# Both feed-forwards of a two-layer diffusion backbone: gate and up as seven block products, activations through DRAM, down summed over all chunks in PSUM

## The chip, the cores and the metric

The kernel runs on one core of a Trainium2 chip. A core has a matrix engine, TensorE (PE), three elementwise engines, VectorE (DVE), ScalarE (ACT) and GpSimd (POOL), and an engine, SyncE (SP), whose queue issues all DMAs of this kernel. The metric is the device time of one execution in microseconds; the median of the runs counts.

## What is computed

The reference has two layers over 512 latent tokens and 256 context tokens of width 1024. Layer 0 mixes the tokens by differential attention, layer 1 by grouped-query attention; only the latent tokens are the output, so layer 1 has no feed-forward for the context. All numbers are float32. What matters here:

```python
def modulate(t, shift, scale):
    return t * (1 + scale) + shift

def swiglu(t, w_gu, w_down):
    gate, up = jnp.split(t @ w_gu, 2, axis=-1)
    return (jax.nn.silu(gate) * up) @ w_down
...
        mod = (cond_lat @ ada_w[i] + ada_b[i])[:, None, :]
        modc = (cond_ctx @ ada_w[i] + ada_b[i])[None, None, :]
        sh1, sc1, g1, sh2, sc2, g2 = jnp.split(mod, 6, axis=-1)
...
        x = x + g1 * y
        x = x + g2 * swiglu(modulate(rmsnorm(x, norm2_g[i]), sh2, sc2), ffn_w_gu[i], ffn_w_down[i])
        if not last:
            xc = xc + cg1 * yc
            xc = xc + cg2 * swiglu(modulate(rmsnorm(xc, norm2_g[i]), csh2, csc2), ffn_w_gu[i], ffn_w_down[i])
```

The hidden width is 2816, which is 22 chunks of 128.

## The kernel before

**Number format.** Each float32 operand of a large product is split into a high part (a cast to fp32r) and a low part (the rest), and a product is three matmuls: high x high, high x low, low x high (mm3, L99). So each weight that comes from DRAM is cast by ACT and subtracted by POOL (split, L85: guh/gul for gate and up, dh/dl for down, woh/wol for the output projection). Names that end in h or l are high and low parts.

**Order.** A scheduler sets the order of every engine's instructions from the program; each engine then works through its own queue in that order. Raw weights land in a pool of three buffers (rawp, 8 KB in each partition), which gate/up, down, output-projection and adaLN weights share; SP issues their loads in order.

**Attention's end in layer 0.** The heads' outputs (po) are normed on ACT, DVE, POOL and, for the mean, PE (pm). Six of eight heads are spilled to DRAM and read back (ol), cast and split into oT0. The first half of the output projection's weights is split ahead of the attention's end, and the sums over the six spilled heads for four of the six token blocks (pso0p) are made early, copied to SBUF (pac) and added later; then come the sums pso. After the last column half of a token block is added to x (L365), norm_a, norm_t (transposes pt on PE) and norm_m (L312; modulation on DVE L322 and ACT L324, cast L327, low part L328) give the transposed, modulated tokens h2 (h3 in layer 1).

**Feed-forward (ffn, L369).** The loop runs over chunks. stage (L419) loads 1 MB of gate and up columns and splits it. gu_mm (L426) multiplies: for gate and for up, 8 blocks of 128 rows, three matmuls each, that is 48 weight blocks of 128x128, each against 512 latent columns (psgu) and, in layer 0, 256 context columns (psgc). ACT applies silu, DVE multiplies by up (L479), ACT casts, DVE takes the low part (L493); the activations a stay in SBUF. Every two chunks (PIECE) down (L375) makes, for each token block and each half of the 1024 columns, six matmuls into a bank psd; DVE multiplies it by the gate (L386, xd) and adds it to x (L387). That is 11 pairs of chunks x 12 sums in layer 0 and x 8 in layer 1, 220 evictions of two operations.

**adaLN of layer 1.** Its scale and shift vectors are sums over 1024 rows, made on DVE in layer 0's feed-forward: 16 operations at L223 and 112 at L225, 128x512 each (adacc<-adaw), one column block at a time between the products (ada_job, L395). Those of layer 0 for the second half of the layer are made on PE (ps_ada) inside the attention.

## Time and profile before

| | us |
|---|---|
| runs: median (lowest to highest of 3) | 1748.15 (1746.62 to 1748.38) |
| span of the profiled execution | 1742.5 |
| PE busy in it | 1657.0 (95%) |
| DVE busy | 1237.5 (71%) |
| ACT busy | 673.0 (39%) |
| POOL busy | 767.6 (44%) |

The span runs from the first to the last instruction that the profile shows; a run's time is the device's and holds a little more. Matmuls are pipelined: a matmul of 512 columns is recorded with 0.39 us while the next starts 0.23 us after it, so the starts are what is to be read. The feed-forward of layer 0 lies between about 520 and 1137 us of the span, that of layer 1 between about 1365 us and the end.

### The profile page before, as it was taken

The numbers are of one execution on the slowest core, as the hardware profiler recorded it, in microseconds if no ns is written. First come the engines' busy times: TensorE is split into PE (matmuls) and PEld (weight loads), VectorE is DVE, ScalarE is ACT, GpSimd is POOL, SyncE is SP. The second block draws the span as 40 slices with busy tenths as digits, with TensorE's granted clock in tenths as the row PEclk, the third lists the DMA queues.
The fourth block names the chain that finished last, engine by engine and source line by source line (L and its number), as shares of the span: only waits on it lengthen the run. The fifth ranks groups of instructions, "written<-read, shape, count | busy, mean of one in ns | idle before, by whom it ended". The sixth has DMA issues, their size and how long they took to land.

```text
span 1742.5 us, 23575 instructions
## 1 busy us (share of the span) xinstructions
PE 1657.0 (95%) x8934; PEld 1403.6 (81%) x8934; DVE 1237.5 (71%) x2016; ACT 673.0 (39%) x1491; POOL 767.6 (44%) x702
## 2 busy tenths in 40 slices
PE   5899999989998999999999999999999999999998
PEld 2789899975778888887777888778897888888887
DVE  4777888877484488878777555798883467677676
ACT  4667767677444121111211022364673522222120
POOL 2687666664645242223232233174435344354340
PEclk8899999999999999999999999999999999999999
DMA  8311111129523133355333221021203133233311
GB/s 303 102 55 38 46 46 58 34 75 336 195 73 121 49 121 111 107 169 169 122 119 99 73 73 40 25 74 48 73 25 120 36 105 103 73 97 99 95 49 49
DMA packets 162435, 165.81 MB, mean 95 GB/s; under 512 B 5097, under 2 KB 120186, under 8 KB 162322
## 3 DMA queue, kind: packets, MB, share of 16 engines
q1 hardware_dynamic: 162322, 164.31, 29.5%
q8 instruction: 70, 1.15, 0.3%
q14 instruction: 43, 0.35, 0.1%
HBM read 159.81 MB, written 4.48 MB: 94 GB/s over the span
## 4 chain that ended last, share of the span: by engine, by line
PE 68%; DVE 18%; ACT 4%; DMA 4%; POOL 3%; issue 2%; SPq 0%; DVEq 0%; ACTq 0%; POOLq 0%
PE psgu L433 24%; PE psgc L433 5%; PE psd L100 5%; PE psd L102 5%; PE psd L101 5%; DVE adacc L225 3%; DMA adaw<-in_ada_w_dram 3%; PE psp L100 2%; PE psp L102 2%; PE psp L101 2%; DVE adacc L223 2%; DVE x L387 2%; DVE xd L386 1%; PE pso L100 1%; PE pso L102 1%
## 5 line engine op out<-in xcount | busy, mean ns | idle before, releaser
L93 POOL TENSOR_TENSOR gul<-gu,guh 128x2048 fp32r<-128x2048 f32 x44 | 211.6, 4809 | 419.6 <-ACT guh L86 419.6
L386 DVE TENSOR_TENSOR xd<-psd,gate 128x512 f32<-128x512 f32 x220 | 151.1, 687 | 202.7 <-PE psd L102 202.5
L387 DVE TENSOR_TENSOR x<-x,xd 128x512 f32<-128x512 f32 x220 | 274.4, 1249 | 5.5
L86 ACT CAST guh<-gu 128x2048 fp32r<-128x2048 f32 x44 | 83.9, 1906 | 403.8 <-PE psgu L433 234.4
L91 POOL TENSOR_TENSOR dl<-wd,dh 128x1024 fp32r<-128x1024 f32 x44 | 120.9, 2768 | 146.1 <-ACT dh L86 146.1
L433 PE MATMUL psgu<-h3latl,guh 128*128 128x512 f32 (+1 forms) x384 | 144.5, 377 | 1.1 <-POOL h3latl L328 1.1
L433 PE MATMUL psgu<-h3lath,gul 128*128 128x512 f32 (+1 forms) x384 | 144.4, 376 | 0.0
L433 PE MATMUL psgu<-h3lath,guh 128*128 128x512 f32 (+1 forms) x384 | 144.3, 377 | 0.0
L433 PE MATMUL psgu<-h2lath,guh 128*128 128x512 f32 (+1 forms) x368 | 142.1, 386 | 0.0
L433 PE MATMUL psgu<-h2lath,gul 128*128 128x512 f32 (+1 forms) x368 | 141.8, 385 | 0.0
L433 PE MATMUL psgu<-h2latl,guh 128*128 128x512 f32 (+1 forms) x368 | 141.8, 385 | 0.0
L100 PE MATMUL psd<-dh,ah 128*128 128x512 f32 x264 | 106.0, 402 | 16.2 <-DVE xd L386 12.1
L102 PE MATMUL psd<-dh,al 128*128 128x512 f32 x264 | 104.8, 397 | 0.0
L101 PE MATMUL psd<-dl,ah 128*128 128x512 f32 x264 | 104.5, 396 | 0.0
L433 PE MATMUL psgc<-h2ctxh,gul 128*128 128x256 f32 x352 | 100.2, 285 | 0.4 <-POOL gul L93 0.4
L433 PE MATMUL psgc<-h2ctxh,guh 128*128 128x256 f32 x352 | 100.1, 284 | 0.0
L433 PE MATMUL psgc<-h2ctxl,guh 128*128 128x256 f32 x352 | 99.6, 283 | 0.0
L225 DVE SCALAR_TENSOR_TENSOR adacc<-adaw,cond,adacc 128x512 f32<-128x512 f32 x112 | 97.5, 896 | 1.3
L100 PE MATMUL psp<-dwh,h0lath 128*128 128x384 f32 x256 | 88.9, 347 | 7.6 <-DVE vl L97 7.6
L101 PE MATMUL psp<-dwl,h0lath 128*128 128x384 f32 x256 | 88.9, 347 | 0.0
L102 PE MATMUL psp<-dwh,h0latl 128*128 128x384 f32 x256 | 88.8, 347 | 0.0
L433 PEld LDWEIGHTS psgu<-h3latl,guh 128*128 128x128 f32 x384 | 72.2, 188 | 15.8 <-POOL h3latl L328 1.3
(389 smaller groups left out, 4669.1 us busy)
## 6 DMA issues: line engine op xcount, KB each, us to landing
adaw<-in_ada_w_dram SPq DMA_DIRECT2D x48, 1024.0 KB
gu<-in_ffn_w_gu_dram SPq DMA_DIRECT2D x88, 512.0 KB
wd<-in_ffn_w_down_dram SPq DMA_DIRECT2D x22, 1024.0 KB
dw<-in_diff_w_in_dram SPq DMA_DIRECT2D x48, 256.0 KB
x<-in_x_dram SPq DMA_DIRECT2D x8, 512.0 KB
wo<-in_diff_w_out_dram SPq DMA_DIRECT2D x4, 1024.0 KB
gw<-in_gqa_w_in_dram SPq DMA_DIRECT2D x4, 1024.0 KB
wo<-in_gqa_w_out_dram SPq DMA_DIRECT2D x4, 1024.0 KB
```

What stands on the lines that cost most here:

```text
L86: S.copy(hi, src)
L91: G.tensor_sub(lo[:, ns], src[:, ns], hi[:, ns])
L93: G.tensor_sub(lo[:, :, ns], src[:, :, ns], hi[:, :, ns])
L100: PE.matmul(ps, lhi, rhi, start=start, stop=False)
L101: PE.matmul(ps, lhi, rlo, start=False, stop=False)
L102: PE.matmul(ps, llo, rhi, start=False, stop=stop)
L223: V.tensor_scalar(acc, w[:, k, :], c, None, op0=ALU.mult)
L225: V.scalar_tensor_tensor(acc, w[:, k, :], c, acc, op0=ALU.mult, op1=ALU.add)
L386: V.tensor_mul(tmp, ps, gates[g][:, s, cs])
L387: last_v[0] = V.tensor_add(xt[tb][:, cs], xt[tb][:, cs], tmp)
L433: last[0] = PE.matmul(o, w_[:, k, us], act.t[kind][x_].k(k, sl_), start=(k == 0 and x_ == 0 and w_ is whi), stop=(k == KC - 1 and w_ is wlo))
```

## The change

**Gate and up** become ffn_up. The weights of a chunk are four blocks of 512 rows x 128 columns (two halves of the rows, gate and up), and the tokens four blocks as well: two halves of the rows and two halves of the tokens (three blocks of 128 in layer 0, [4, 5, 0] and [1, 2, 3], where 4 and 5 are the context; two in layer 1). In place of eight block products there are seven, each of one weight form with one token form; each is 4 x 3 = 12 matmuls of 384 columns (256 in layer 1). The class Forms makes the token forms b11, b21, b22 and t1 to t4 once; prep makes the weight forms per chunk, by four sums of 128x512 (all on POOL in layer 0, two on POOL and two on DVE in layer 1), a cast on ACT and a low part on DVE for each of the seven. Three forms, t1, t2 and t4, and with them the fifth product of the order, need both halves of the tokens. Products that belong together are added in the same PSUM bank without an eviction between. Weight forms are made six products ahead (LEAD).

**Activations** g1 and g2 (one half of the tokens each) go from SBUF to DRAM (a0, a1). **Down** becomes ffn_down: for one half of the tokens after the other, the sums of all token blocks and column halves stay in PSUM over all 22 chunks, with the activations read back and split, and the down weights loaded and split once for each half; an eviction is made only at the end (12 in layer 0, 8 in layer 1).

**Around it.** The adaLN steps of layer 1 are placed in layer 0's gate and up and in the first half of its down. The buffers of the output projection's weights lie on the other side of SBUF now, over pools that the attention uses to its end.

The core of the diff:

```diff
+    class Forms:
+        def put(self, name, j, src, eng):
+            if name not in self.tiles:
+                self.late.append((name, j, src, eng))
+                return
+            t, cs = self.tiles[name], slice(j * P, j * P + P)
+            S.copy(t[:, 0, :, cs], src)
+            last_v[0] = eng.tensor_sub(t[:, 1, :, cs], src, t[:, 0, :, cs])
...
+            if half == 0:
+                self.put("b11", j, lo, V)
+                self.put("b21", j, hi, G)
+            else:
+                b11, b21 = self.ht[0, j]
+                self.put("b22", j, hi, G)
+                V.tensor_sub(b11, lo, b11)
+                self.put("t1", j, b11, V)
+                V.tensor_sub(lo, hi, lo)
+                V.tensor_sub(hi, hi, b11)
+                self.put("t2", j, hi, G)
+                V.tensor_sub(b21, b21, hi)
+                self.put("t3", j, lo, V)
+                self.put("t4", j, b21, G)
...
-            for k in range(KC):
-                for w_, x_ in ((whi, 0), (whi, 1), (wlo, 0)):
-                    for kind, sl_ in segs:
-                        o = pcx[:, u * CTX : u * CTX + CTX] if kind else plat[:, u, sl_]
-                        last[0] = PE.matmul(
-                            o, w_[:, k, us], act.t[kind][x_].k(k, sl_),
-                            start=(k == 0 and x_ == 0 and w_ is whi), stop=(k == KC - 1 and w_ is wlo))
...
+    RHS = {1: "b11", 2: "b21", 3: "b22", 4: "t4", 5: "t1", 6: "t2", 7: "t3"}
+    LEAD = 6
+    def product_order():
+        o = [(0, 1), (0, 2), (1, 1), (1, 2), (0, 5), (0, 6), (0, 3), (0, 7), (1, 5), (0, 4), (1, 6), (1, 3), (1, 7)]
+        for h in range(2, NHC):
+            o += [(h, 1), (h - 1, 4), (h, 2), (h, 5), (h, 6), (h, 3), (h, 7)]
+        return o + [(NHC - 1, 4)]
...
+            if n == 5:
+                adds[0].tensor_add(s1, r21, r22)
+                adds[1].tensor_sub(r21, r11, r21)
+            elif n == 6:
+                adds[2].tensor_sub(r11, s1, r11)
+            elif n == 3:
+                adds[3].tensor_sub(r12, r12, r11)
+            src = {1: r11, 2: r12, 5: s1, 6: r11, 3: r12, 7: r21, 4: r22}[n]
...
+            S.copy(t[:, 0], src)
+            V.tensor_sub(t[:, 1], src, t[:, 0])
...
+            for k in range(4):
+                for a_, b_ in ((0, 0), (0, 1), (1, 0)):
+                    last_m[0] = PE.matmul(
+                        ps, w[:, a_, k, :], x[:, b_, k, :],
+                        start=(n in (1, 2, 5) and k == 0 and a_ + b_ == 0),
+                        stop=(k == 3 and a_ == 1), skip_group_check=n in (3, 4, 6, 7))
...
+            if n == 1:
+                S.copy(c1, ps)
+            elif n == 2:
+                V.tensor_add(g1, ps, c1)
+                S.activation(g1, g1, AF.Silu)
...
+            elif n == 7:
+                V.tensor_add(u2, ps, c5)
+                last_v[0] = V.tensor_mul(g2, g2, u2)
+                put(hc, 1, g2)
+            else:
+                last_v[0] = V.tensor_mul(g1, g1, ps)
+                put(hc, 0, g1)
...
+    def ffn_down(l, xt, halves, g, a_dram, a_tile, banks, lo_eng, step, after):
...
+                if k % 4 == 0:
+                    n = min(4, NHC - k)
+                    r = raw_tile(f"ar{l}_{half}_{k}", 4, th)[:, :n]
+                    dma(r, a_dram[k : k + n, :, half, :].rearrange("k p n -> p k n"))
+                    t = a_tile(half, k).rearrange("p (x k n) -> p x k n", x=2, k=4)
+                    S.copy(t[:, 0, :n], r)
+                    V.tensor_sub(t[:, 1, :n], r, t[:, 0, :n])
...
+                S.copy(t[:, 0], ww["raw"][:, k % 2])
+                lo_eng.tensor_sub(t[:, 1], ww["raw"][:, k % 2], t[:, 0])
...
-    s2 = ctx.enter_context(tc.tile_pool(name="s2", bufs=1, side="right", reuse_waits="tile"))
-    pools.update(w=(s2, 4), f=(s2, 1))
     es.close()
     ape_es.close()
+    xtp = ctx.enter_context(tc.tile_pool(name="xtp", bufs=2, reuse_waits="tile"))
+    s1 = ctx.enter_context(tc.tile_pool(name="s1", bufs=1, reuse_waits="tile"))
+    pools.update(x=(s1, 2), xc=(s1, 1), gate=(s1, 1), w=(s1, 4))
...
+    ffn_up(
+        0, F0, lambda hc: evp.tile([P, 6 * TH], F32, tag="ev", name=f"ev0_{hc}"), lambda hc: st0[:, hc % 2],
+        a0, (G, G, G, G), lambda i: ada_step() if i > 14 and i % 2 and i < 130 else None, lambda i: None)
...
+    def step0(half, k):
+        ada_bank[0] = "TP"[half]
+        ada_step(2)
```

**What moves: PE at the attention's end.** The rows are PE's order from the last products po of the last head on; ps_ada and ps_adag are layer 0's adaLN, pm the mean of the last head's norm, pso0p the partial output projection. Before:

```order
L100 MATMUL po_5_5805<-aTh_4_5775,vh_5_4969 128x256
L101 MATMUL po_5_5805<-aTl_4_5776,vh_5_4969 128x256
L102 MATMUL po_5_5805<-aTh_4_5775,vl_5_4970 128x256
L102 MATMUL pso0p_6081<-woh_5856,oT0ctxl 128x512
L100 MATMUL pso0p_6081<-woh_5856,oT0ctxh 128x512
```

Now:

```order
L102 MATMUL po_5_5805<-aTh_4_5775,vl_5_4970 128x256
L245 MATMUL ps_ada_5_5993<-adaw_5_0_5994,cond 32x512 x4
L835 MATMUL pm_5833<-sq_5831,ones_m 128x384 x2
L245 MATMUL ps_ada_5_5993<-adaw_5_1_6000,cond 32x512 x4
L211 MATMUL ps_adag_5_6010<-adaev_5_6006,selcol 2x512
L245 MATMUL ps_ada_10_6014<-adaw_10_0_6015,cond 32x512 x4
L245 MATMUL ps_ada_10_6014<-adaw_10_1_6021,cond 32x512 x4
L211 MATMUL ps_adag_10_6031<-adaev_10_6027,selcol 2x512
L245 MATMUL ps_ada_11_6035<-adaw_11_0_6036,cond 32x512 x4
L245 MATMUL ps_ada_11_6035<-adaw_11_1_6042,cond 32x512 x4
L211 MATMUL ps_adag_11_6052<-adaev_11_6048,selcol 2x512
L100 MATMUL pso0p_6090<-woh_5865,oT0ctxh 128x512
```

Before, pso0p stands among the last heads' products and right behind them; now the adaLN blocks 5, 10 and 11 and the norm's mean stand between the last po and the first pso0p.

**POOL at the same place.** mt is the last head's norm, oT0ctxl and oT0latl the low parts of the heads (those from ol are spilled heads, those from o_5696 the last one), wol the low parts of the output projection's weights. Before:

```order
L91 TENSOR_TENSOR oT0latl_5408<-ol_6047,oT0lath_5406 128x512 x2
L91 TENSOR_TENSOR oT0latl_5408<-ol_6058,oT0lath_5406 128x512 x2
L811 TENSOR_TENSOR mt_5836<-mt_5836,sq_5831 128x768
L812 TENSOR_TENSOR mt_5836<-mt_5836,sq_5831 128x768
L91 TENSOR_TENSOR oT0latl_5409<-o_5696,oT0lath_5407 128x512
L91 TENSOR_TENSOR oT0ctxl<-o_5696,oT0ctxh 128x256
L93 TENSOR_TENSOR wol_6288<-wo_6285,woh_6287 128x2x256 x4
L93 TENSOR_TENSOR wol_6298<-wo_6295,woh_6297 128x2x256 x4
```

Now:

```order
L847 TENSOR_TENSOR mt_5836<-mt_5836,sq_5831 128x768
L848 TENSOR_TENSOR mt_5836<-mt_5836,sq_5831 128x768
L91 TENSOR_TENSOR oT0latl_5409<-o_5696,oT0lath_5407 128x512
L91 TENSOR_TENSOR oT0ctxl<-o_5696,oT0ctxh 128x256
L93 TENSOR_TENSOR wol_5866<-wo_5863,woh_5865 128x2x256 x4
L93 TENSOR_TENSOR wol_5876<-wo_5873,woh_5875 128x2x256 x4
L91 TENSOR_TENSOR oT0latl_5408<-ol_6056,oT0lath_5406 128x512
L91 TENSOR_TENSOR oT0ctxl<-ol_6056,oT0ctxh 128x256
L91 TENSOR_TENSOR oT0latl_5408<-ol_6056,oT0lath_5406 128x512
L91 TENSOR_TENSOR oT0ctxl<-ol_6056,oT0ctxh 128x256
```

Before, the spilled heads stood ahead of the last head's norm, and the wol that follows is the second column half's; now the first half's wol stands behind the last head, and the spilled heads behind that.

**DVE in layer 0's feed-forward.** Rows from the middle of the chunks; adacc is layer 1's adaLN, al an activation's low part, wf the low part of a weight form, ev the eviction of a product (L467, L474). Before:

```order
L493 TENSOR_TENSOR al_2_7478<-sil_6831,ah_2_7477 128x768
L387 TENSOR_TENSOR x_6170<-x_6170,xd_1_4_0_7492 128x512
L225 SCALAR_TENSOR_TENSOR adacc_1_1_7404<-adaw_1_0_7405,cond,adacc_1_1_7404 128x512
L386 TENSOR_TENSOR xd_1_4_1_7502<-psd_1_4_1_7495,gate_7076 128x512
L225 SCALAR_TENSOR_TENSOR adacc_1_0_7403<-adaw_1_1_7415,cond,adacc_1_0_7403 128x512
L225 SCALAR_TENSOR_TENSOR adacc_1_1_7404<-adaw_1_1_7415,cond,adacc_1_1_7404 128x512
L387 TENSOR_TENSOR x_6170<-x_6170,xd_1_4_1_7502 128x512
L386 TENSOR_TENSOR xd_1_5_0_7512<-psd_1_5_0_7505,gate_7076 128x512
L225 SCALAR_TENSOR_TENSOR adacc_1_0_7403<-adaw_1_1_7415,cond,adacc_1_0_7403 128x512
L225 SCALAR_TENSOR_TENSOR adacc_1_1_7404<-adaw_1_1_7415,cond,adacc_1_1_7404 128x512
L387 TENSOR_TENSOR x_6170<-x_6170,xd_1_5_0_7512 128x512
```

Now:

```order
L1026 SCALAR_TENSOR_TENSOR adacc_2_0_7669<-adw_4_7827,cond,adacc_2_0_7669 128x512
L1026 SCALAR_TENSOR_TENSOR adacc_2_1_7670<-adw_4_7827,cond,adacc_2_1_7670 128x512
L1026 SCALAR_TENSOR_TENSOR adacc_2_0_7669<-adw_4_7827,cond,adacc_2_0_7669 128x512
L1026 SCALAR_TENSOR_TENSOR adacc_2_1_7670<-adw_4_7827,cond,adacc_2_1_7670 128x512
L1026 SCALAR_TENSOR_TENSOR adacc_2_0_7669<-adw_6_7901,cond,adacc_2_0_7669 128x512
L438 TENSOR_TENSOR wf_5_6_7325<-gu_5_7115,wf_5_6_7325 128x512
L1026 SCALAR_TENSOR_TENSOR adacc_2_1_7670<-adw_6_7901,cond,adacc_2_1_7670 128x512
L474 TENSOR_TENSOR ev_4_7253<-psc_4_7310,ev_4_7253 128x384
L1026 SCALAR_TENSOR_TENSOR adacc_2_0_7669<-adw_6_7901,cond,adacc_2_0_7669 128x512
L438 TENSOR_TENSOR wf_5_6_7325<-gu_5_7115,wf_5_6_7325 128x512
L1026 SCALAR_TENSOR_TENSOR adacc_2_1_7670<-adw_6_7901,cond,adacc_2_1_7670 128x512
L467 TENSOR_TENSOR ev_5_7400<-psu_5_7399,ev_5_7400 128x384
```

Before, the adaLN sums stood between evictions of down and additions to x; now they stand between low parts of weight forms, for which the products of gate and up wait. All 90 of those in gate and up stand ahead of the weight form of the 73rd of 154 products.

## Rows read from the trace of the kernel before

**Rows 1.** The page: busy time by engine (share, instructions); slices, GB/s; chain.

```profile
PE 1657.0 (95%) x8934; PEld 1403.6 (81%) x8934; DVE 1237.5 (71%) x2016; ACT 673.0 (39%) x1491; POOL 767.6 (44%) x702
...
GB/s 303 102 55 38 46 46 58 34 75 336 195 73 121 49 121 111 107 169 169 122 119 99 73 73 40 25 74 48 73 25 120 36 105 103 73 97 99 95 49 49
...
PE 68%; DVE 18%; ACT 4%; DMA 4%; POOL 3%; issue 2%; SPq 0%; DVEq 0%; ACTq 0%; POOLq 0%
```

**Rows 2.** Stretches of 50 us: engines' busy us (instructions), granted clock, DMA share, GB/s.

```profile
500.00:550.00 50.00, 43.84 (x271) 39.66 (x270) 35.41 (x69) 30.05 (x67) 26.96 (x12) 0.93 0.30 92
1450.00:1500.00 50.00, 50.00 (x216) 40.22 (x215) 35.78 (x30) 12.92 (x13) 24.33 (x7) 1.00 0.28 84
```

**Rows 3.** Timeline of PE (start us, length us), feed-forward of layer 0; 24 such rows.

```profile
540.76 0.28 PE L433 MATMUL psgu<-h2lath,guh 128*128 128x256 f32 x1
...
543.49 0.29 PE L433 MATMUL psgu<-h2lath,gul 128*128 128x256 f32 x1
```

**Rows 4.** Timeline of PE, projections of layer 0's attention; 11 such rows.

```profile
79.73 0.34 PE L102 MATMUL psp<-dwh,h0latl 128*128 128x384 f32 x1
...
81.46 0.33 PE L100 MATMUL psp<-dwh,h0lath 128*128 128x384 f32 x1
```

**Rows 5.** Waits of PE in layer 0's feed-forward: us in total, times, longest.

```profile
PE psd L100 <- DVE xd L386: 11.1, 8, 2.2
PE psd L100 <- DVE mod L241: 4.1, 2, 2.7
```

**Rows 6.** Timeline of DVE and of POOL: what one operation takes.

```profile
445.12 1.01 DVE L848 TENSOR_TENSOR aTl<-pat,aTh 128x384 fp32r<-128x384 f32 x2
...
513.68 0.69 DVE L365 TENSOR_TENSOR x<-x,xo 128x512 f32<-128x512 f32 x1
...
531.49 1.25 POOL L328 TENSOR_TENSOR h2latl<-xs01g,h2lath 128x512 fp32r<-128x512 f32 x1
...
703.60 2.07 DVE L225 SCALAR_TENSOR_TENSOR adacc<-adaw,cond,adacc 128x512 f32<-128x512 f32 x3
```

**Rows 7.** Timeline of POOL (one row) and of DVE beside it, layer 1's feed-forward.

```profile
1456.97 4.66 POOL L93 TENSOR_TENSOR gul<-gu,guh 128x2048 fp32r<-128x2048 f32 x1 [14.98 <-ACT guh L86]
...
1457.28 0.69 DVE L386 TENSOR_TENSOR xd<-psd,gate 128x512 f32<-128x512 f32 x1 [3.25 <-PE psd L102]
1457.89 0.68 DVE L479 TENSOR_TENSOR sil<-sil,psgu 128x512 f32<-128x512 f32 x1
1458.48 3.70 DVE L387 TENSOR_TENSOR x<-x,xd 128x512 f32<-128x512 f32 x1
```

**Rows 8.** Groups by line: form xcount | busy us, mean ns | idle before them.

```profile
L387 DVE TENSOR_TENSOR x<-x,xd 128x512 f32<-128x512 f32 x220 | 274.4, 1249 | 5.5
L91 POOL TENSOR_TENSOR dl<-wd,dh 128x1024 fp32r<-128x1024 f32 x44 | 120.9, 2768 | 146.1 <-ACT dh L86 146.1
...
L93 POOL TENSOR_TENSOR wol<-wo,woh 128x512 fp32r<-128x512 f32 x32 | 43.9, 1405 | 15.2 <-ACT woh L86 15.1
```

**Rows 9.** Timeline, end of layer 0's attention: PE, DVE, POOL.

```profile
449.56 0.28 PE L102 MATMUL po<-aTh,vl 128*128 128x256 f32 x1
...
468.14 0.39 PE L100 MATMUL pso<-woh,oT0lath 128*128 128x512 f32 x1
...
466.05 1.02 DVE L818 SCALAR_TENSOR_TENSOR o<-o,sub_col,sq 128x768 f32<-128x768 f32 x1
...
455.56 0.74 POOL L91 TENSOR_TENSOR oT0ctxl<-o,oT0ctxh 128x256 fp32r<-128x256 f32 x1
```

**Rows 10.** Timeline, entry of layer 0's feed-forward: PE, DVE, ACT.

```profile
533.67 1.97 PE L307 MATMUL pt<-ident,xs01f 128*128 128x128 f32 x8 [4.87 <-DVE m_n L112]
536.93 1.33 PE L307 MATMUL pt<-ident,xs01f 128*128 128x128 f32 x5 [1.29 <-DVE xs01f L322]
...
524.04 0.73 DVE L365 TENSOR_TENSOR x<-x,xo 128x512 f32<-128x512 f32 x1
...
538.94 1.50 ACT L324 ACTIVATE xs01f<-pt,mod,modA 128x128 f32<-128x128 f32 x4 [0.73 <-PE pt L307]
```

More of the change, by code (lines that the diff above doesn't have):

```diff
@@ L407, in load @@
         def load(hc):
-            if hc < NHC:
-                w = wraw[hc] = raw_tile(f"gu{l}_{hc}", KC, 256)
+            if hc < NHC and hc not in raw:
+                w = raw[hc] = raw_tile(f"gu{l}_{hc}", KC, 256)
                 for u in range(2):
```

395 lines of the change are left out of this document (215 added, 180 removed).

## The prediction

> **What bounds the kernel now.** I read the engine totals first [rows 1]: TensorE (PE) is busy for 1657.0 of 1742.5 us, and 68% of the chain that ended last is its own. In a typical 50 us of layer 1's feed-forward [rows 2] it is never idle: 216 matmuls of 512 columns, 0.2315 us from start to start. Two runs of starts give the other widths: 23 steps of 256 columns in 2.73 us, 0.1187 us each [rows 3], and 10 steps of 384 columns in 1.73 us, 0.173 us each [rows 4]. So a matmul's time goes with its columns, and fewer columns are fewer microseconds as long as nothing else ends last. Next to PE stand two waits in layer 0's feed-forward [rows 5]: 11.1 and 4.1 us ahead of down products, for DVE. Then I read the two elementwise engines, since the change hands them new work. A subtraction of 128x512 takes GpSimd (POOL) 1.25 us and DVE 0.69 [rows 6], 0.61 from start to start where two follow each other [rows 7]. But the two do not run freely side by side [rows 7]: POOL began a 128x2048 subtraction at 1456.97 and needed 4.66 us; DVE ran two operations that read PSUM inside it, 0.69 and 0.68 us, and then x<-x,xd, with both inputs in SBUF, took 3.70 us and ended with POOL's. This is why the 220 of L387 average 1249 ns [rows 8].
>
> **What the change removes.** Per chunk and layer, 48 weight blocks against all tokens become 84 against half of them. Layer 0: 22 x 48 x (0.2315 + 0.1187) = 369.8 us becomes 22 x 84 x 0.173 = 319.7, **-50.1**. Layer 1: 22 x 48 x 0.2315 = 244.5 becomes 22 x 84 x 0.1187 = 219.4, **-25.1**. The down products keep their number and width. Their 220 evictions become 20, as each sum stays in its bank until all 22 chunks are in; the waits of [rows 5], 11.1 + 4.1, go: **-15.2**. Together **-90.4**.
>
> **What it adds, place by place.** (A) *End of the attention.* Before, the weights of the output projection were split early, and the partial sums pso0p began before the last po; from the last po to the first pso are 18.6 us [rows 9]. Now ACT casts these weights only behind the last head's cast, POOL subtracts eight pieces of wol ahead of six spilled heads, and PE has adaLN's blocks 5, 10 and 11 between the last po and the first pso0p. My walk: the last head's norm ends some 15 us after its po (16.5 now [rows 9], a little of it behind POOL's spilled heads), 2 us for its low parts, 8 x 1.4 = 11.2 for wol [rows 8], 6 x 2.0 = 12 for the spilled heads (1.25 + 0.74 [rows 6, 9]), and 18 matmuls of 512 behind them, 4.2: 44.4 against 18.6, less the time of the moved adaLN blocks, which stood inside the attention: 24 matmuls of 512 columns at the 0.2315 of [rows 2], an estimate of 5.6. **+20**; 15 if POOL finds room for wol during the norm, 34 if the last adaLN loads come one by one, as only three raw buffers hold them.
>
> (B) *Entry of layer 0's feed-forward.* From DVE's last residual add to ACT's last modulation are 14.9 us now, and PE idles 4.9 and 1.3 us in it [rows 10]. The fifth product needs t1 and POOL's weight form st, which stands on POOL's queue behind nine form subtractions of 1.25 us. I add 5.5 us for DVE's nine form operations after the last transpose, and 5.5 for the half of POOL's work that falls behind them: 26. PE's cover is four products, 4 x 12 x 0.173 = 8.3, and the transposes, 1; 16.7 idle against 6.2: **+10**; 4 if POOL keeps up, 25 if each of its operations also stops DVE.
>
> (C) *Gate and up of layer 0.* By product 76 of 154, DVE's order holds 72 low parts of weight forms (0.61, 44 us), 90 adaLN accumulations (three in 2.07 us [rows 6], 62) and some 50 evictions of 384 columns (two in 1.01 us [rows 6], 25): 131 us, where PE needs 71 x 2.08 = 147. POOL has 41 additions in that stretch. If they cost DVE nothing, nothing is lost; if each keeps DVE out for its 1.25 us, 131 + 51 = 182, and PE is 35 us late. Four evictions of five read PSUM and can run inside a POOL operation, as in [rows 7]; POOL gets in while one of them runs, so I take 1.25 - 0.5 = 0.75 each, 131 + 31 = 162, **+15**, 0 to 35. Behind product 76 adaLN is gone from DVE's queue: 7 x 0.61 + 5 x 0.5 + 4 x 0.75 = 9.8 us a chunk against PE's 14.5, so the loss comes once.
>
> The Trainium skill, SBUF — State Buffer, section "SBUF: two separate sides", says that a GpSimd operation and a DVE operation with two SBUF inputs take their shared ports as an exclusive lock for the whole instruction. The 3.70 us of [rows 7] agree with it. By that sentence alone the price in C would be its upper end, the second rival's.
>
> (D) *Down of layer 0, first half.* For four chunks (72 matmuls, 16.7 us) SP loads 0.8 MB of stored activations, 2.1 MB of weights and 2.1 MB of adaLN weights: 300 GB/s. The densest slices of the page moved 303 and 336 [rows 1], others that load much 195, and all go through three raw buffers. **+8**, 0 to 20.
>
> (E) *Entry of layer 1's feed-forward*, like B, with a cover of 4 x 12 x 0.1187 = 5.7 us but only two blocks in the second half: **+8**, 4 to 15. (F) *Gate and up of layer 1*: DVE 9 x 0.61 (two weight sums are its own) + 5 x 0.4 = 7.5 us a chunk, and two POOL operations, 1.5 to 2.5, against PE's 84 x 0.1187 = 9.97: it just fits, **+2**, 0 to 12. (G) *Down of layer 1*: POOL subtracts one 128x1024 block a chunk, 2.77 us [rows 8], for 12 matmuls, 2.78: at the edge, **+4**, 0 to 15. Activations are stored and read back a phase apart, which hides it. What is left are the ends of the phases (first down weights behind the last forms, the change of halves) and a lower granted clock after longer idle time (0.93 in the 50 us around today's entry [rows 2]): **+8**, 3 to 15.
>
> Sum: 20 + 10 + 15 + 8 + 8 + 2 + 4 + 8 = 75 against 90.4, **-15.4**. The span of the profiled execution is 1742.5; the median of the runs is 5.6 above it, which I keep: 1742.5 - 15.4 + 5.6 = 1732.7, say **1733**.
>
> **Rivals.** *First: the covers hold.* DVE has 16 us of slack up to product 76, and weight forms are made six products ahead, so a POOL operation that falls into DVE's gaps costs nothing: C, D, F and G at 0, A 15, B and E 4 each, the ends 3: 26 lost, 1684. For it: PE ends last nearly everywhere now [rows 1]. Against: in the rows shown DVE stands still when POOL works [rows 7].
>
> *Second, the slower one: the lock between POOL and DVE sets the pace.* Place: DVE's queue in both up phases and at layer 0's entry. If every POOL operation keeps DVE out for its whole length, C is 35, B 25 and F 12, 45 more than forecast: 1778. Since 15.4 of these 45 bring the sum to zero, it decides from a third of the way on, at 0.92 us per POOL operation in place of 0.75. For it: four fifths of DVE's time up to product 76 are operations with two SBUF inputs. Against: evictions that let POOL in come four to a chunk, as many as POOL's operations.
>
> *Third: the queues behind the attention eat it*: A 34 and the ends 15, the rest as forecast, 21 more: 1754. For it: PE's order holds nothing else there; against: the ACT and POOL work in that place is short.
>
> *That the change does not do what it says* is excluded: the order has 22 x 84 matmuls of 384 columns, and as many of 256.
>
> **How the numbers follow.** A measurement of this kernel tells about 0.2%, 3.5 us, from no change. Chances: forecast 0.53, in a band of 1712 to 1754 (0.40 faster, 0.07 within, 0.06 slower); covers hold 0.19, faster; lock 0.20, slower; queues 0.08 (0.03 within, 0.05 slower). Faster 0.59, same 0.10, slower 0.31. For 8 times in 10 the range goes from 1684, the first rival's time, to 1775, a little short of the second's; about 0.1 is left out on each side. The forecast's own band is the middle of it.
>
> **What would show it.** PE's starts 0.173 and 0.119 us apart in the up phases, and no wait of psd for xd: the gain. PE idle for some 25 us more between the last po and the first pso: A. In layer 0's up phase, PE waits for a weight form's low part (DVE, L438) that stop by product 80: C; if they go on, or come in layer 1's up phase, the lock is worse than I took it. PE waits for ar or wd loads: D. I am wrong if PE idles much in places not named here, or if DVE's operations stay at their short times beside POOL's and the run is below 1684.

## The result and the profile after

The changed kernel takes 1812.42 us (1809.67 to 1817.7, 4 runs), the kernel before, on the same chip, 1747.38 (1745.28 to 1748.38, 4 runs): a ratio of 1.0374, 95% interval 1.0354 to 1.0393. It is slower by 65 us where 15 less were forecast, and it lies above the range. The profiled execution spans 1811.1 us, 68.6 more than before.

The page of the changed kernel: busy time by engine, GB/s in 40 slices, and the chain that ended last.

```profile
PE 1626.6 (90%) x9318; PEld 1440.5 (80%) x9318; DVE 1202.9 (66%) x2127; ACT 870.0 (48%) x1948; POOL 873.8 (48%) x844
...
GB/s 292 106 46 36 45 45 56 33 99 175 285 70 47 107 162 153 205 96 96 101 134 183 184 206 168 140 94 47 71 24 47 10 131 117 117 117 146 233 232 157
...
PE 8%; DVE 5%; DMA 2%; POOL 2%; issue 1%; ACT 1%; ACTq 0%; SPq 0%; DVEq 0%
```

Beside [rows 1]: PE has less to do, but its share fell from 95 to 90%. DVE's sum fell as well; ACT and POOL rose by 197 and 106 us. The chain, PE's for 68% before, is here followed over a small part of the span only (the shares above sum to 18%), so I read stretches instead.

Stretches of 50 us of the changed kernel, columns as in [rows 2]:

```profile
450.00:500.00 50.00, 28.50 (x91) 11.11 (x92) 4.87 (x6) 14.40 (x25) 27.91 (x26) 0.62 0.81 287
...
550.00:600.00 50.00, 29.61 (x139) 26.37 (x137) 43.80 (x70) 27.99 (x60) 28.61 (x20) 0.80 0.14 43
...
800.00:850.00 50.00, 50.00 (x288) 50.00 (x287) 28.46 (x42) 21.02 (x42) 20.36 (x14) 1.00 0.32 94
...
950.00:1000.00 50.00, 41.14 (x159) 31.61 (x158) 25.21 (x20) 11.49 (x11) 21.28 (x9) 0.86 0.53 181
1000.00:1050.00 50.00, 42.51 (x165) 31.11 (x163) 27.73 (x19) 10.94 (x10) 18.13 (x8) 0.93 0.57 199
1050.00:1100.00 50.00, 40.12 (x149) 30.11 (x148) 34.96 (x35) 14.74 (x20) 25.01 (x10) 0.86 0.55 184
1500.00:1550.00 50.00, 47.25 (x388) 46.19 (x387) 41.95 (x69) 25.64 (x56) 11.90 (x8) 1.00 0.46 132
```

The row at 800 is the gain as planned: 288 matmuls of 384 columns in 50 us, 0.174 us each, and PE never stands. The others are the losses: the end of the attention (450), the entry of layer 0's feed-forward (550), the down products of layer 0's first half (950 to 1100) and gate and up of layer 1 (1500), where 388 matmuls in 50 us are 0.129 us each, not 0.119. In the first three places the granted clock is down as well.

To place the 68.6 us, I took the starts of all matmuls from both traces, and from each stage's length the number of its matmuls times their normal distance (0.2315, 0.173, 0.1187 us by width). What is left is PE's idle time, a slower clock included. In the kernel before, most down products stand between those of gate and up, so rows C and D are to be read together:

| stage | idle before | idle after | growth | forecast |
|---|---|---|---|---|
| start to first pso of layer 0 (A) | 78.1 | 117.2 | +39.1 | +20 |
| on to the 9th product of gate and up, before to 545 us (B) | 12.6 | 38.1 | +25.5 | +10 |
| rest of gate and up, layer 0 (C, less the 15.2 of [rows 5]) | 28.6 | 21.5 | -7.1 | -0.2 |
| down of layer 0 (D) | 5.0 | 47.2 | +42.2 | +8 |
| attention of layer 1 | 25.0 | 30.5 | +5.5 | 0 |
| entry, gate and up of layer 1 (E, F) | 8.2 | 39.8 | +31.6 | +10 |
| down of layer 1 (G) | 0.3 | 5.7 | +5.4 | +4 |
| phase ends, clock | | in the above | | +8 |
| **sum** | 157.7 | 300.1 | **+142.4** | **+59.8** |

The rest, 68.6 - 142.4 = -73.8, is matmul time saved, against -75.2 forecast. This part is counted and not measured: it is the number of matmuls times their distance. The measured part is the distance itself, 0.174 us in the row at 800. So what went wrong is idle time. Waits of PE in the whole run of the changed kernel (us in total, times, longest):

```profile
PE ps_ada L245 <- DMA adaw<-in_ada_w_dram: 25.4, 15, 6.5
PE pt L291 <- DVE xs L278: 21.6, 6, 7.3
PE psu L459 <- ACT ev L465: 12.6, 1, 12.6
...
PE ps_adar L232 <- DVE adacc L1026: 9.2, 3, 4.1
PE psu L459 <- DVE ev L481: 8.0, 9, 1.0
PE ps_adac L220 <- DVE adacc L1026: 7.7, 5, 3.7
```

No wait of psd for xd is left, as forecast. The waits for evictions of layer 1 (L481, F) are new; those for adaLN's loads (A) and for adaLN's sums (D) were 2.4 and 0.4 us before.

### The profile page after: what moved, and what is told of

It reads as the page before. It is cut to its first block, busy times and chain, and to the rows that moved or that the text cites. A ratio compares the mean times of both kernels' runs of the same rounds, so it can differ in the third digit from the quotient of the medians.

```text
span 1811.1 us, 25754 instructions
## 1 busy us (share of the span) xinstructions
PE 1626.6 (90%) x9318; PEld 1440.5 (80%) x9318; DVE 1202.9 (66%) x2127; ACT 870.0 (48%) x1948; POOL 873.8 (48%) x844
## 5 line engine op out<-in xcount | busy, mean ns | idle before, releaser
L438 DVE TENSOR_TENSOR wf<-gu,wf 128x512 fp32r<-128x512 f32 x264 | 217.0, 839 | 63.7 <-ACT wf L437 63.4
L437 ACT CAST wf<-gu 128x512 fp32r<-128x512 f32 x264 | 156.3, 618 | 176.8 <-PE psu L459 142.1
L459 PE MATMUL psu<-hf0t,wf 128*128 128x384 f32 x792 | 154.4, 345 | 11.7 <-DVE ev L467 4.6
L459 PEld LDWEIGHTS psu<-hf0t,wf 128*128 128x128 f32 x792 | 142.5, 192 | 13.8 <-DVE ev L467 5.7
L1026 DVE SCALAR_TENSOR_TENSOR adacc<-adw,cond,adacc 128x512 f32<-128x512 f32 x112 | 123.8, 1117 | 25.2 <-DMA adw<-in_ada_w_dram 23.7
L459 PE MATMUL psu<-hf0b,wf 128*128 128x384 f32 x528 | 102.9, 344 | 12.9 <-ACT ev L465 12.6
L459 PEld LDWEIGHTS psu<-hf0b,wf 128*128 128x128 f32 x528 | 95.3, 194 | 13.4 <-ACT ev L465 12.8
L459 PE MATMUL psu<-hf1t,wf 128*128 128x256 f32 x792 | 102.9, 284 | 0.8 <-ACT hf1t L332 0.8
L459 PEld LDWEIGHTS psu<-hf1t,wf 128*128 128x128 f32 x792 | 98.2, 190 | 1.7 <-ACT hf1t L332 1.1
L868 ACT ACTIVATE p<-pS,mx 128x768 f32<-128x768 f32 (+1 forms) x96 | 73.8, 771 | 13.3 <-DVE mx L867 12.8
```

The costliest lines, as they stand in the source:

```text
L437: S.copy(t[:, 0], src)
L438: V.tensor_sub(t[:, 1], src, t[:, 0])
L459: last_m[0] = PE.matmul(ps, w[:, a_, k, :], x[:, b_, k, :], start=(n in (1, 2, 5) and k == 0 and a_ + b_ == 0), stop=(k == 3 and a_ == 1), ...
L868: S.activation(p[i][:, :n], s, AF.Exp, bias=mx[:, i : i + 1], accum_out=l_[:, i : i + 1])
L1026: V.scalar_tensor_tensor(acc, w[:, k, :], c, acc, op0=ALU.mult, op1=ALU.add)
```

## Experiments

The theory after the result had two parts. At the end of the attention, layer 0's last adaLN weights come late because the output projection's raw weights hold two of the three raw buffers. In the feed-forwards, POOL and DVE hinder each other: a DVE operation with two SBUF inputs doesn't proceed while POOL works (the lock). The rivals to these: ACT's and POOL's own queues at the attention's end (as in my forecast), and the loads, the adaLN sums or mere dependences in the feed-forwards. All ratios are to the kernel before; differences in us are between medians.

### 1. The end of the attention

Timeline of the changed kernel there, PE (start, length, [idle before]) and ACT:

```profile
460.54 1.51 PE L245 MATMUL ps_ada<-adaw,cond 128*32 128x512 f32 x8 [2.74 <-DMA adaw<-in_ada_w_dram]
467.23 1.94 PE L245 MATMUL ps_ada<-adaw,cond 128*32 128x512 f32 x8 [5.18 <-DMA adaw<-in_ada_w_dram]
...
478.30 1.93 PE L245 MATMUL ps_ada<-adaw,cond 128*32 128x512 f32 x8 [6.51 <-DMA adaw<-in_ada_w_dram]
483.47 1.93 PE L245 MATMUL ps_ada<-adaw,cond 128*32 128x512 f32 x8 [3.23 <-DMA adaw<-in_ada_w_dram]
...
464.12 3.88 ACT L86 CAST woh<-wo 128x1024 fp32r<-128x1024 f32 x4
```

The output projection's weights (wo) are loaded at 292.7 us, but their casts run only at 464.12, so two raw buffers are held for 171 us, and adaLN's blocks come through the third, 1 MB at a time; between the last po and the first pso PE waits 18.8 us for them in five places.

e1_wo_late makes the same split, but behind those adaLN loads in the program:

```diff
-    o_weights(wt, wtags, dw_out[0], "0", 0)
...
+    o_weights(wt, wtags, dw_out[0], "0", 0)
```

> The changed kernel, with the loads and splits of the output projection's first half of weights (wo) placed behind the adaLN blocks and the spilled heads in program order. Theory, raw buffers: in the changed kernel wo is loaded at 293 us and its two raw buffers are held until ACT reads them at 464 us, so that the adaLN weights go through the one that is left, a megabyte at a time. Then this kernel's stretch from the last po to the first pso falls from 60.5 us to 33 to 42, the waits of ps_ada for adaw (25.4 us in all) mostly go, and the run comes out at 1785 to 1795. Rival, the walk of the prediction (ACT and POOL queues behind the last head, 44 us): the stretch stays at 44 or more, run at 1797 or above. Second rival, DMA bandwidth (14 MB go through in these 50 us anyway): it stays above 50, run above 1802.

Measured: 1786.84 us, ratio 1.0218 (1.0175 to 1.0261), 25.6 below the changed kernel; from the last po to the first pso 39.8 us in place of 60.5. PE's timeline there:

```profile
456.06 1.56 PE L835 MATMUL pm<-sq,ones_m 128*128 128x384 f32 x4 [3.04 <-ACT sq L828]
471.39 1.22 PE L100 MATMUL pso0p<-woh,oT0ctxh 128*128 128x512 f32 x2 [13.77 <-ACT woh L86]
```

The waits for adaLN are gone there; one of 13.77 us for ACT's cast of woh stands in their place. The stretch and the run came out as the theory had them. But of the 20.7 us by which the stretch is shorter, 12.5 are adaLN's own matmuls, which now run ahead of the last po; 8.2 are idle time. From the start to the first pso, the row A of the table, idle time falls by 14.7 us. So the held buffers are some 14.7 of the 39.1 us that A had grown by, and 24.4 stay; the time to the last po alone varies by up to 6 us from run to run (below).

### 2. The feed-forwards: which side of the collision

Timeline of the changed kernel in the first half of layer 0's down, DVE and POOL:

```profile
957.11 4.72 DVE L1026 SCALAR_TENSOR_TENSOR adacc<-adw,cond,adacc 128x512 f32<-128x512 f32 x2 [3.97 <-DMA adw<-in_ada_w_dram]
965.83 1.54 DVE L1026 SCALAR_TENSOR_TENSOR adacc<-adw,cond,adacc 128x512 f32<-128x512 f32 x2 [4.01 <-DMA adw<-in_ada_w_dram]
...
984.42 7.09 DVE L1026 SCALAR_TENSOR_TENSOR adacc<-adw,cond,adacc 128x512 f32<-128x512 f32 x4 [1.26 <-DMA adw<-in_ada_w_dram]
...
956.06 2.42 POOL L511 TENSOR_TENSOR wd_4x<-wd,wd_4x 128x1024 fp32r<-128x1024 f32 x1 [1.08 <-ACT wd_4x L510]
958.42 2.86 POOL L511 TENSOR_TENSOR wd_5x<-wd,wd_5x 128x1024 fp32r<-128x1024 f32 x1
...
984.26 2.38 POOL L511 TENSOR_TENSOR wd_8x<-wd,wd_8x 128x1024 fp32r<-128x1024 f32 x1 [10.03 <-ACT wd_8x L510]
986.60 2.79 POOL L511 TENSOR_TENSOR wd_9x<-wd,wd_9x 128x1024 fp32r<-128x1024 f32 x1
```

Two adaLN sums take 1.54 us where POOL is idle (965.83; its next operation starts at 969.51) and 4.72 where it is not (957.11). Of the 32 such sums behind gate and up, 19 meet no POOL operation and take 0.75 us on average, 13 do and take 2.63; in e4 below, all 32 take 0.75. Both engines read raw buffers here, so a late sum or a late low part also makes the next load late.

e2_adds_v moves the sums of the weight forms from POOL to DVE, e4_lo_v the low parts of the down weights; e3_no_sums leaves out layer 1's adaLN sums but for the first of each block and single columns, so that layer's scales, shifts and gates are not computed in full.

e2_adds_v:

```diff
-        a0, (G, G, G, G), lambda i: ada_step() if i > 14 and i % 2 and i < 130 else None, lambda i: None)
+        a0, (V, V, V, V), lambda i: ada_step() if i > 14 and i % 2 and i < 130 else None, lambda i: None)
...
-        1, F1, lambda hc: slab("l", F32, f"ev1_{hc}"), lambda hc: st1[:, hc % 4], a1, (G, G, V, V),
+        1, F1, lambda hc: slab("l", F32, f"ev1_{hc}"), lambda hc: st1[:, hc % 4], a1, (V, V, V, V),
```

e3_no_sums:

```diff
-                        else:
-                            V.scalar_tensor_tensor(acc, w[:, k, :], c, acc, op0=ALU.mult, op1=ALU.add)
+                        elif k == 0:
+                            V.tensor_scalar(acc[:, 0:1], w[:, k, 0:1], c, None, op0=ALU.mult)
```

e4_lo_v:

```diff
-        (("S", "S", "P"), ("T", "S", "S")), G, step0, after0)
+        (("S", "S", "P"), ("T", "S", "S")), V, step0, after0)
...
-        (("S", "S"), ("P", "T")), G, lambda half, k: None, store)
+        (("S", "S"), ("P", "T")), V, lambda half, k: None, store)
```

> The changed kernel with all four sums of a chunk's weight forms on DVE in both layers (in the changed kernel four on POOL in layer 0, two of four in layer 1). Theory, lock: a POOL sum of 1.25 us or more keeps DVE's two-input operations out for longer than the 0.61 us that DVE needs to do the sum itself. Then gate and up of layer 1 (1445 to 1675) gets shorter by 12 to 18 us, its matmuls come 0.119 us apart instead of 0.129, that of layer 0 loses 5 to 12 us of its 21 us of idle, and the run is 1785 to 1797. Rival, plain load: DVE is the busier engine (42 of 50 us in layer 1's up), so 2 or 4 more operations a chunk make it slower, layer 1 by 2 x 0.61 x 22 = 27 us at most, layer 0 up to 10, run 1820 to 1850.

> The changed kernel without nearly all of layer 1's adaLN sums: of each column block's 8 operations per stream only the first is made in full, in the others DVE reads one column; the loads stay. The values of layer 1's modulation are therefore not the reference's. Theory, DVE's adaLN work is what delays weight forms in layer 0's up and PE's adaLN products in its down: idle time of PE in the up (612 to 940) falls from about 21 us to under 8, the waits of ps_adac and ps_adar for adacc (16.9 us) and the lower clock behind them go from the down; run 1770 to 1785. Rival, loads and raw buffers set the down and POOL's sums the up: up -5, down under -10, run about 1800.

> The changed kernel with the low parts of the down weights on DVE instead of POOL, in both layers. Theory, POOL's 2.4 to 2.8 us for a 128x1024 block is at the edge against 12 matmuls (2.78 us) in layer 1 and in the way of DVE in layer 0: layer 1's down -3 to -5, layer 0's -3 to -8, run 1800 to 1806. Rival, loads set the pace of the down, and DVE gets 1.2 us more a chunk in front of the adaLN sums: within 3 us of 1812, or up to 5 longer.

Measured, with idle time by stage as above:

| | us | ratio (95%) | 4th to 9th product, L0 | 9th to 76th | down L0 | gate and up L1 |
|---|---|---|---|---|---|---|
| changed kernel | 1812.42 | 1.0374 | 10.2 | 19.2 | 47.2 | 37.4 |
| e2_adds_v | 1775.58 | 1.0154 (1.0111 to 1.0197) | 0.2 | 8.1 | 47.0 | 28.2 |
| e3_no_sums | 1767.96 | 1.011 (1.0073 to 1.0148) | 3.0 | 10.0 | 20.2 | 35.9 |
| e4_lo_v | 1772.56 | 1.0137 (1.0107 to 1.0166) | 10.3 | 21.8 | 12.7 | 35.1 |

DVE gets more work in e2 and e4, and both runs become shorter, by 36.8 and 39.9 us. In the profiled runs some 6 us of e2's are no effect of its edit: the last po of the attention, which it doesn't touch, came at 440.9 us in place of 446.7. The sizes were not foreseen: gate and up of layer 1 was to gain 12 to 18 us in e2 and gained 9.2, and down of layer 0 was to gain 3 to 8 in e4. e4 takes 34.5 of the 47.2 us out of down, e3, which leaves POOL as it is, 27.0: either side of the collision gives most of it back, so neither the loads nor the number of sums alone is the cause. Groups of DVE, for the changed kernel, for e2, for e4 and for e5_three (below, both moves at once), as one form, xcount | busy us, mean ns:

```profile
L438 DVE TENSOR_TENSOR wf<-gu,wf 128x512 fp32r<-128x512 f32 x264 | 217.0, 839 | 63.7 <-ACT wf L437 63.4
...
L1026 DVE SCALAR_TENSOR_TENSOR adacc<-adw,cond,adacc 128x512 f32<-128x512 f32 x112 | 123.8, 1117 | 25.2 <-DMA adw<-in_ada_w_dram 23.7
```

```profile
L438 DVE TENSOR_TENSOR wf<-gu,wf 128x512 fp32r<-128x512 f32 x264 | 176.4, 684 | 16.4 <-ACT wf L437 15.9
```

```profile
L1026 DVE SCALAR_TENSOR_TENSOR adacc<-adw,cond,adacc 128x512 f32<-128x512 f32 x112 | 100.0, 905 | 14.7 <-DMA adw<-in_ada_w_dram 13.2
```

```profile
L1026 DVE SCALAR_TENSOR_TENSOR adacc<-adw,cond,adacc 128x512 f32<-128x512 f32 x112 | 82.6, 744 | 7.0 <-DMA adw<-in_ada_w_dram 6.3
```

Without POOL beside it the low part takes 684 ns, as the 0.69 us of [rows 6]; with it 839, 41 us more over the group. Without POOL's low parts beside them adaLN's sums fall from 1117 to 905 ns, and without its weight sums as well to 744.

### 3. The price of one POOL operation

In the runs above POOL's results were also waited for, and POOL needs longer for an operation than DVE; these runs alone can't tell that from the lock. e9_idle_pool is e8_ada_up (below), a version without POOL work in the feed-forwards, plus four POOL subtractions per chunk in layer 1's gate and up, whose results nobody waits for:

```diff
+        def idle_pool(n, w):
+            if l == 1 and n in (5, 6, 3, 7):
+                G.tensor_sub(scr_ref[0].rearrange("p (k n) -> p k n", k=4), gates[1, 1][:, 0, 0:512].rearrange("p (k n) -> p k n", k=4), w[:, 0])
...
             w, x = wform.pop((hc, n)), F.tiles[RHS[n]]
+            idle_pool(n, w)
```

> As e8_ada_up, and in layer 1's gate and up four POOL subtractions of 128x512 per chunk (88 in all), each of which reads one weight form and writes a spare tile that nobody reads. Nothing waits for a result of theirs, so a queue or a dependence can't explain a loss; only what POOL and DVE share can. The stage (first to last product of layer 1's gate and up) took 248.9 us in e8_ada_up, and DVE was busy 79% of it, 8 us of the 10 us that a chunk's products take. Theory (POOL and a DVE operation with two SBUF inputs don't run at the same time): per chunk 4 x 1.25 = 5 us more in which DVE's 7 low parts and 4 weight sums stand still, less what falls under its evictions from PSUM, so 11 to 13 us in place of 10: the stage grows by 22 to 65 us, the run to 1735 to 1780, and the low parts of the weight forms (0.61 to 0.84 us before) average over 1 us there. Rival (what went with the POOL operations in the earlier runs was only that DVE had to wait for their results): the stage stays within 5 us of 248.9 and the low parts keep their length.

Measured: 1762.56 us, ratio 1.0075 (1.0052 to 1.0097), 49.4 above e8_ada_up. The stage grew from 248.9 to 301.4 us, its idle time from 26.2 to 78.7. Groups of DVE between 1343 and 1592 us, first e8_ada_up, then e9_idle_pool, with POOL's group of the same stage below it:

```profile
L439 DVE TENSOR_TENSOR wf<-gu,wf 128x512 fp32r<-128x512 f32 x128 | 85.9, 684 | 5.8 <-ACT wf L438 5.3
...
L468 DVE TENSOR_TENSOR ev<-psu,ev 128x256 f32<-128x256 f32 x22 | 9.2, 419 | 6.4 <-PE psu L460 6.4
```

```profile
L440 DVE TENSOR_TENSOR wf<-gu,wf 128x512 fp32r<-128x512 f32 x112 | 107.1, 968 | 1.4 <-ACT wf L439 1.1
...
L474 DVE TENSOR_TENSOR ev<-psu,ev 128x256 f32<-128x256 f32 x19 | 7.9, 416 | 2.0 <-PE psu L466 2.0
...
L444 POOL TENSOR_TENSOR scr<-gate,wf 128x512 f32<-128x512 f32 x88 | 150.4, 1710 | 202.2 <-ACT wf L439 129.2 <-issue 69.6
```

One place of the stage, DVE and POOL in e9_idle_pool:

```profile
1450.83 1.78 DVE L440 TENSOR_TENSOR wf<-gu,wf 128x512 fp32r<-128x512 f32 x1
1452.53 0.41 DVE L488 TENSOR_TENSOR ev<-ev,psu 128x256 f32<-128x256 f32 x1
...
1457.45 0.68 DVE L440 TENSOR_TENSOR wf<-gu,wf 128x512 fp32r<-128x512 f32 x1
...
1448.62 6.82 POOL L444 TENSOR_TENSOR scr<-gate,wf 128x512 f32<-128x512 f32 x4 [3.25 <-ACT wf L439]
1460.61 1.82 POOL L444 TENSOR_TENSOR scr<-gate,wf 128x512 f32<-128x512 f32 x1 [5.17 <-ACT wf L439]
```

The low parts went from 684 to 968 ns, just short of the 1 us of the theory, and the evictions that read PSUM stayed at 419 and 416. Within this one run, the 57 low parts that meet no POOL operation take 0.68 us on average, the 71 that do 1.23. 52.5 us over 88 operations are 0.60 us each. One dependence is left in it: two ACT casts waited 4.2 us together for a weight form that POOL still read. The rival (dependences alone) falls. DVE's share in e8_ada_up was 83% over the whole stage (207 of 249 us); the 79% of the expectation is that of the 50 us from 1500 on.

Two SBUF inputs are not the only condition. The first sum of an adaLN block scales one SBUF tile into another; in the changed kernel eight of these 16 take 0.47 to 0.49 us, and the eight that start while POOL works 0.88 to 2.21:

```profile
972.31 2.21 DVE L1024 TENSOR_SCALAR adacc<-adw,cond 128x512 f32<-128x512 f32 x1 [4.94 <-DMA adw<-in_ada_w_dram]
...
971.85 2.39 POOL L511 TENSOR_TENSOR wd_7x<-wd,wd_7x 128x1024 fp32r<-128x1024 f32 x1
```

### 4. The same exchange in the kernel before

b1_split_v moves the low parts of the feed-forwards' weights (128x2048 and 128x1024) from POOL to DVE in the kernel before:

```diff
-            split(whi, wlo, wraw[hc])
+            split(whi, wlo, wraw[hc], eng=V)
...
-                    split(wd[0][:, ci, :], wd[1][:, ci, :], wr[:, ci, :])
+                    split(wd[0][:, ci, :], wd[1][:, ci, :], wr[:, ci, :], eng=V)
```

> The kernel before, with the low parts of all feed-forward weights (128x2048 and 128x1024) on DVE instead of POOL. It tells whether the lock alone costs the old order something. Theory, lock: the 220 of L387 fall from 1249 to about 700 ns, the waits of psd for xd and mod (15.2 us) get shorter by a half or more, run 1730 to 1742. Rival: the old kernel hides all this under PE (it waited 15 us in all), and DVE, at 71%, takes on 44 operations of some 2.3 and 44 of some 1.2 us, in stretches without a gap; the waits stay or grow, run 1745 to 1765.

Measured: 1736.77 us, ratio 0.9929 (0.9914 to 0.9944). The additions to x, that group of the trace, beside the first of [rows 8]:

```profile
L388 DVE TENSOR_TENSOR x<-x,xd 128x512 f32<-128x512 f32 x220 | 153.7, 700 | 4.8
```

1249 became 700 ns, and the wait of psd for xd fell from 11.1 us [rows 5] to 2.6, as the theory had it; waits of 6.9 us for ACT's casts guh are new. So POOL's work beside DVE had a price before too: moving it is worth 12.6 us of the run, and PE hid the rest.

### 5. Together

e5_three is e1, e2 and e4 in one; e6_three_forms moves the last four token-form low parts (b21, b22, t2, t4) to DVE as well.

> The changed kernel with the three edits that gave 26 (wo late), 37 (sums of the weight forms on DVE) and 40 us (low parts of the down weights on DVE) one by one. Theory: the first is a wait for raw buffers, the two others are the lock between POOL and DVE at different places (gate and up; down of layer 0), so they add up but for little: 1812 - 103 = 1709, taken as 1705 to 1720, faster than the kernel before (1747). Rival: what POOL gave up makes DVE the bound in layer 0's down, where the adaLN sums are, or idle time moves to the next wait: 1725 to 1745.

> As e5_three, and the low parts of the token forms b21, b22, t2 and t4 on DVE as well, so that POOL has no work from the start of layer 0's feed-forward to its end but what the norms give it. Theory, lock at the entry: DVE's chain of forms loses the 1 to 1.2 us that each of nine POOL operations adds to a DVE operation (569.32 took 1.77, 573.89 took 1.82 us instead of 0.69), but gets nine of 0.61 instead: entry of layer 0 shorter by 2 to 6 us, of layer 1 by 1 to 3. Rival: DVE is busy without a gap at the entry, and 9 x 0.61 us more in its queue put the fifth product later by 3 to 6 us.

Measured: 1727.7 us, ratio 0.9879 (0.9862 to 0.9896), and 1724.53, 0.9862 (0.9846 to 0.9878). The three edits gave 25.6, 36.8 and 39.9 apart, 102.3 in sum, and 84.7 together. So they don't add up as the theory had it (1705 to 1720); the time falls into the rival's range (1725 to 1745), and some 15 us of idle time are left in down of layer 0. e6 is 3.2 us below e5, and their runs overlap; layer 0's idle time up to the 4th product is some 3 us shorter, layer 1's entry is not. In e5 the entry between the 4th and 9th product has 0.2 us of idle time, and one stretch of layer 1's gate and up reads:

```profile
1400.00:1450.00 50.00, 49.55 (x415) 49.20 (x414) 43.18 (x83) 27.71 (x60) 0.00 (x0) 1.00 0.45 128
```

415 matmuls in 50 us, 0.120 each, against 388 with 11.90 us of POOL beside them (the row at 1500 above), with DVE slightly busier.

e7_w_first gives the output projection's split weights memory of their own, so that their casts don't wait for the last head, and has DVE make their low parts. e8_ada_up puts an adaLN step at two of three products, up to the end of gate and up, so that hardly any are left in down.

```diff
+    sw = ctx.enter_context(tc.tile_pool(name="sw", bufs=1, reuse_waits="tile"))
...
-    pools.update(x=(s1, 2), xc=(s1, 1), gate=(s1, 1), w=(s1, 4))
+    pools.update(x=(s1, 2), xc=(s1, 1), gate=(s1, 1), w=(sw, 4))
...
-        a0, (V, V, V, V), lambda i: ada_step() if i > 14 and i % 2 and i < 130 else None, lambda i: None)
+        a0, (V, V, V, V), lambda i: ada_step() if i > 14 and i % 3 and i < 160 else None, lambda i: None)
```

> As e6_three_forms, with the buffers w (weights of the output projection, later the weight forms) first in the memory that the attention gives back, and the output projection's low parts on DVE. Theory, place in memory: in e6 ACT casts woh only behind the last head's cast, since w lies over what the last head's norm still reads; PE waits 13.6 us for it and 2.4 us for POOL's wol. In this kernel's order woh's casts stand ahead of that cast. Then last po to first pso goes from 38.3 to 24 to 30 us, run 1711 to 1718. Rival: the wo loads (457 to 464 us there) or the last head's norm end last anyway: 33 us or more, run 1719 or above.

> As e7_w_first, with 93 of the 96 adaLN steps in layer 0's gate and up (58 before), so that its down has three raw buffers for stored activations and down weights alone. Theory, raw buffers in the down: PE's waits for wd's casts there (9 us in e5) go, the up has room on DVE behind product 76, 1703 to 1712 or 6 to 9 us below e7. Rival: the 35 steps more on DVE delay weight forms by as much or more: at e7 or up to 10 us above it.

Measured: 1719.69 us, ratio 0.9823 (0.9802 to 0.9844), and 1713.18, 0.978 (0.9757 to 0.9803). In e7 the way from last po to first pso takes 32.6 us (38.3 in e6), not the 24 to 30 of the theory, and as the last po comes 4.1 us later, the first pso comes only 1.6 earlier; what gave the rest of its 4.8 us I didn't take apart. e8 is 6.5 us below e7, as expected: in it the idle time in down of layer 0 is gone (-0.8, so within the error of this reckoning), for 7.4 us more of it in gate and up. The last is the fastest kernel of this study, 37 us below the kernel before: the seven products pay once POOL is out of DVE's way and the loads no longer hold each other's buffers. The kernel before gains 12.6 us by part of the same exchange (b1); against that version it is 23.6 us.

## Why the prediction was wrong

**Removed (-90.4): right.** The columns gave -73.8 (forecast -75.2), and the 15.2 us of [rows 5] are gone. This reckoning finds some 13 us more of idle time around them before, most of it in steps too small to be listed as waits, which I hadn't counted.

**A (+20, measured +39.1): right place, wrong step.** I walked through ACT's and POOL's queues; what stood last was SP's loads (18.8 of the 30 us that PE idles from the last po to the first pso). I had this mechanism, three raw buffers and adaLN one load at a time, but only as the upper end, 34, since I looked at what the change adds to ACT and POOL and not at how long a load that is issued early keeps its buffer. e1 shows it: 14.7 us of A. Of the 24.4 that stay, 13.77 are the wait for woh in that run; ACT's cast there stands behind the last head, as in my walk, but its load is also issued only then (456.97), so the two aren't told apart. One term had the wrong size: the 24 moved adaLN matmuls, taken off with 5.6 us, are 48 rows in the trace, eight in 1.94 us (467.23 above), so 11.6. With that my walk gives 14 in place of 20. The clock adds some 2 us: it is 0.62 in the stretch at 450, and the first products behind the gaps start slower.

**B (+10, measured +25.5): two causes, one priced too low.** The 10.2 us between the 4th and the 9th product were POOL beside adaLN's sums (0.2 in e2, 3.0 in e3): there my upper end, "each of its operations also stops DVE", is what happened. e2 alone wouldn't show it, as it also takes the weight form st off POOL's queue; e3 leaves that queue and takes 7.2 of the 10.2. Of the 17.0 from the first to the 4th, 15.1 are left in e6. PE's longest wait there is the 12.6 us for ACT's eviction L465, and this eviction waits for a token form, though it doesn't read one. ACT's row in the changed kernel's timeline:

```profile
589.58 0.86 ACT L465 COPY ev<-psu 128x384 f32<-128x384 f32 x2 [1.87 <-POOL hf0t L333]
```

By the program the tile ev lies on memory of the norm's tiles, from which the last forms are made; this was read and not tried.

**C (+15, measured 21.5 idle in all): right in place and near in size.** Of it 19.2 lie ahead of product 76 and 2.3 behind, as I had it ("the loss comes once"). e2 takes 11.1 us out of it, 0.27 for each of POOL's 41 operations in that stretch; e3 takes 9.2 out. The 0.27 can't be held against the 0.75 I took: that was DVE's loss ahead of 16 us of slack, and e2 has DVE do the sums itself, at 0.61 us each. In the terms of the forecast, 19.2 us of idle time and 16 of slack over 41 operations would be 0.86 each, if all of it were POOL's, which no run shows.

**D (+8, measured +42.2): the step that failed.** I priced the loads, by bytes, and left POOL out, though the change doubles the low parts of the down weights and sets 128x1024 subtractions of 2.77 us [rows 8] beside adaLN's sums. Before, those sums had the long matmuls of gate and up as cover and no one waiting for them soon. Now PE's queue holds the adaLN products (ps_adac, ps_adar) between the down products, and the raw buffers are freed late by both engines. What the runs showed in place of the bytes: beside POOL an adaLN sum takes 2.63 us and not 0.75 (13 of 32), and with the low parts on DVE 34.5 of the 47.2 us are gone (e4), with the sums left out 27.0 (e3). The bytes were not the limit: the slices that lie in this phase moved 140 to 206 GB/s, where 285 were reached at the attention's end, and e4 moves the same bytes with 12.7 us left. They go when adaLN's loads and sums leave the phase (e8).

**E and F (+10, measured +31.6): both terms too small.** 9.2 of it go when POOL's 44 sums move to DVE (e2), 0.21 us each, with DVE's own time for them paid. Behind the 9th product, which is F, 17.0 us are idle where I had 2, at most 12; 6.9 of the 9.2 lie there. The larger part is the entry, E: of 20.5 us of idle time up to the 9th product 16.5 are left in e8_ada_up, and DVE is busy in all 20 us of this stretch of it:

```profile
1340.00:1360.00 20.00, 7.97 (x57) 6.93 (x56) 20.00 (x42) 13.78 (x31) 0.00 (x0) 0.85 0.00 0
```

So DVE's own work is the bound there, not POOL's: some 9.5 us of these 20 are operations of token forms, 8.7 those of the first weight forms, the rest the norm's and two evictions. I had put the token forms at 5.5 us in B and at less in E, and hadn't counted the first weight forms. This is read from the profile; no run made that work shorter. In the second half of gate and up 7.9 us are idle, 7.3 still in e8_ada_up, so POOL isn't their cause; half of them are waits for evictions (L481 here, L468 in e8).

**G (+4, measured +5.4): right**; at the edge, as said, and 0.5 to 0.9 us of idle time in the versions with DVE's low parts.

**The attention of layer 1 (+5.5)** wasn't in the forecast. The rotary table and the gates share a slab that the down evictions now need to the end of layer 0; a wait of 6.0 us for gaTw and one for the first values stand there. I didn't test it, so this cause stays open. The time from the start to the last po also moves from run to run: in the changed kernel, e2, e3 and e4 every engine has the same order of operations up to there (by the names of the tiles), and the last po starts at 446.7, 440.9, 446.6 and 444.0 us (454.1 in e8 and 447.9 in e9, whose order is the same too). So differences of 6 us between two versions are not worth explaining by their edit.

**The rivals.** The slower one, the lock, is the one that came, and it came further: 1812 where it gave 1778. But its place was wrong in the main. I named gate and up and layer 0's entry. In layer 0's gate and up idle time came out near the forecast and under the rival's 35 us; at layer 0's entry 10.2 us are its, and in layer 1's gate and up 6.9 of 17.0. Most of it lay in down of layer 0, where neither the forecast nor this rival had POOL. And it isn't all of the loss: with the buffers freed (e1), moving POOL's work gives 59.1 us (e1 to e5); A's rest and DVE's own forms at both entries stay. "Queues behind the attention" had the place of A, not its cause. My chance for slower, 0.31, was too low, since I took terms as independent that have one cause: POOL beside DVE appears in B, C, D and F, and what is too low in one is likely too low in the others.
